# Rotary angles and half of the mask work moved from VectorE to GpSimd in a two-layer decoder trunk

## The chip, the cores and the metric

The kernel runs on one core of a Trainium2 chip. The metric is the device time of one execution in microseconds (us), the median of several runs. The engines are named as the profile names them: PE is TensorE (its matmuls; PEld its weight loads), DVE is VectorE, ACT is ScalarE, POOL is GpSimd, SP the engine whose queue issues most of the DMAs. Each engine works through its own queue in order and waits on semaphores of the others.

## The reference

256 tokens of width 1024 pass through two layers. Each layer is, cut to what matters:

```python
mod = silu(c) @ w_ada + b_ada              # shift, scale, gate
h   = rms_norm(x, pre_g) * (1 + scale) + shift
proj = h @ w_in                            # q k v g of branch A, q k v g of branch B
q, k = apply_partial_rope(q, cos, sin)     # first 16 of 64 head dims, angle = position * inv_freq
o   = attention(q, k, v) * silu(g)         # A: dilated windows mixed; B: causal at this length
x   = x + gate * rms_norm(concat(o_a, o_b) @ w_out, post_g)
```

All arithmetic is float32. The rotary angles come from integer positions up to some 4,350, and the cosines and sines are shared by both layers. Branch A adds to its scores a mask that counts in how many of three dilated windows a key lies; branch B adds a causal mask. Both masks depend on nothing but the distance of query and key.

## The kernel before

**Tiling.** 128 tokens are one tile (t = 0, 1); the width 1024 is eight blocks of 128. Every float32 matrix product is made of three products of rounded parts: a weight piece `raw` (128 x 1024, 512 KB, seven buffers) is loaded by SP, rounded to `whi` on ACT (L205), and the rest `wlo = raw - whi` is formed on DVE in two instructions of 128 x 512 (L212). The activations have `hi` (ACT) and `lo` (DVE) in the same way. A `raw` buffer is loaded again when its readers are done.

**Order.** Up to the end of the first part of layer 0 the order of all engines is that of the program text (`manual_schedule`), and the string FIRST_STEPS sets it: each word is a step. The steps that matter here:

- `n0`, `n1` (`first_norm`, L698): sum of squares of a token tile on ACT (L702), reciprocal root on POOL in two instructions (L462, L465), scaling on DVE (L704) into `oo` (tile 0) or `acc_ss` (tile 1).
- `T0` (`small_inputs`, L273): one PE transpose (L275) of the small inputs into a PSUM tile `t`, from which ACT makes `cs` = silu(c) (L276) and DVE makes `csz`, `posf` (positions) and `cols` (L277 to L279).
- `x0`, `x1` (`first_x`, L707): eight PE transposes of a scaled token tile (L712), in two groups of four into one PSUM tile each, and the copies of the two tiles on ACT (L713). For token tile 0 the PSUM tiles are of the name `t`, of which there are two buffers.
- `k3`, `k1` (`keep_clock`, L793): three matmuls, or one, of 128 x 512 whose result nobody reads (L797).
- `a0`, `m0`: matmuls of w_ada for a group of columns (L414), the copy on ACT (L418), two or four transposes (L370), and shift and scale `mod` on DVE (L426, L375, L376); `a1`, `m1` and so on for the next groups.
- `h10`, `l10` and so on (`first_h`, `first_lo`): `hf` on DVE (L724), `hi` on ACT (L726), `lo` on DVE (L734). `g02`: the two L212 halves of a piece in part. `p02`: six matmuls of w_in (L753). `w00`, `y00`: splits of whole pieces. `s00`, `v00`: matmuls on those (L513).
- `R0`, `R1`, `R2` (`make_rope`, L284): R0 fills two small constants on POOL (L288, L292: 8 and 9 memsets of one column) and forms the angles of the positions, 7 instructions on DVE (L296 to L302, 128 x 16); R1 reduces them to turns, 18 instructions on DVE (L307 to L324, 128 x 16 to 128 x 48); R2 is four Sin instructions on ACT (L328 to L331). The results are first read where q and k of layer 0 are taken out of PSUM (L547).
- `K1` (`make_masks`, L252 to L258): eight DVE instructions of 128 x 384 that finish the masks `mka` and `mkb`. The first part of the masks (L246 to L250) is made on DVE before the first norm. The masks are first read at L601, after st_S of the first head pair.

From there on PE's order is written out and the other engines' order comes from the scheduler.

Of the kernel before, what the change touches and what calls it, by code (L numbers as in the profile page):

```python
# [21 lines left out]
BIG = 1e30  # L22
# [20 lines left out]

GROUPS = ((0, 1), (1, 1), (2, 2), (4, 2), (6, 2))
FIRST_LOADS = 'a0 f01 f00 a1 s00 b2 a2 f10 s01 f11 v00 a3 b3 v01 f20 a4 f21 f30 b4 f31'
FIRST_STEPS = """n0 T0 R0 k3 n1 x0 R1 k1 a0 f00 f01 x1 m0 h00 h01 l00 g00 l01 g01 a1 f02 m1 p00 f03 p01 h10 h11 l10
g02 R2 l11 g03 p02 w00 s00 a2 b2 m2 p03 f10 h20 h21 g10 l20 l21 f11 f12 g11 s02 f13 g12 g13 w01 K1
p10 p11 a3 s01 s03 p12 y00 y01 b3 p13 m3 f20 h30 h31 l30 g20 f21 l31 v00 f22 f23 g21 g22 g23 v01 p20
p21 a4 f30 g30 f31 g31 b4 p22 m4 p23 h40 h41 l41 l40 v02 f32 f33 v03 g32 g33 p30 p31 p32 p33"""
GATE_AT = (21, 27)  # L50
# [24 lines left out]
def trunk(ctx: ExitStack, tc: tile.TileContext, x, c, positions, pre_gain, post_gain,  # L75
          w_ada, b_ada, w_in, w_out, out):
    nc = tc.nc
# [4 lines left out]
    NT = S // P  # L82
# [85 lines left out]
    for x in FIRST_LOADS.split():  # L168
        i, g, m = x[0], int(x[1]), int(x[2:] or 0)
# [67 lines left out]
    def make_masks():  # L237
        dist = ap.tile([P, NS], I32, name="z", bufs=4)
        nc.gpsimd.iota(dist[:, 0:P], pattern=[[-1, P]], base=0, channel_multiplier=1)
        nc.gpsimd.iota(dist[:, P:NS], pattern=[[-1, S]], base=P, channel_multiplier=1)  # L240
        d = dist
        mka, mkb = masks
        tmi = ap.tile([P, NS], I32, name="z", bufs=4)
        tmf = ap.tile([P, NS], F32, name="z", bufs=4)
        cnt = ap.tile([P, NS], F32, name="z", bufs=4)
        nc.vector.tensor_scalar(cnt, d, 128.0, None, op0=ALU.is_le)  # L246
        for m in (3, 15):
            nc.vector.tensor_scalar(tmi, d, m, None, op0=ALU.bitwise_and)
            nc.vector.tensor_scalar(tmf, tmi, 0.0, None, op0=ALU.is_equal)
            nc.vector.tensor_add(cnt, cnt, tmf)  # L250
        yield
        nc.vector.tensor_scalar(mkb, d, 0.0, BIG, op0=ALU.is_lt, op1=ALU.mult)  # L252
        nc.vector.tensor_scalar(tmf, d, 0.0, None, op0=ALU.is_ge)
        nc.vector.tensor_mul(cnt, cnt, tmf)
        nc.vector.tensor_scalar(mka, cnt, 0.0, BIG, op0=ALU.is_equal, op1=ALU.mult)
        for v in (2, 3):
            nc.vector.tensor_scalar(tmf, cnt, float(v), -math.log(v), op0=ALU.is_equal, op1=ALU.mult)
            nc.vector.tensor_add(mka, mka, tmf)  # L258
        yield

# [23 lines left out]
    def make_rope():  # L284

        invf = cp.tile([P, RH], F32, name="invf")
        for i in range(RH):
            nc.gpsimd.memset(invf[:, i:i + 1], INV_FREQ[i])  # L288
        tcn = cp.tile([P, 3, 3], F32, name="tcn")
        for j, r in enumerate(turn_constants()):  # L290
            for i in range(3):
                nc.gpsimd.memset(tcn[:, i, j:j + 1], r[i])  # L292
        NA = NT * RH
        ang = cp.tile([P, 4, NA], F32, name="ang")
        pcs = cp.tile([P, 3, NA], F32, name="pcs")
        nc.vector.tensor_mul(ang[:, 0, :].rearrange("p (t i) -> p t i", t=NT),  # L296
                             posf[:, :, None].to_broadcast([P, NT, RH]),
                             invf[:, None, :].to_broadcast([P, NT, RH]))
        for j, e in enumerate((20, 8, -4)):
            mg = 1.5 * 2.0 ** (23 + e)  # L300
            nc.vector.tensor_scalar(pcs[:, j, :], ang[:, j, :], mg, mg, op0=ALU.add, op1=ALU.subtract)
            nc.vector.tensor_sub(ang[:, j + 1, :], ang[:, j, :], pcs[:, j, :])  # L302
        yield
        RND = 1.5 * 2.0 ** 23
        tp = cp.tile([P, 3, 3, NA], F32, name="tp")
        for i in range(3):
            nc.vector.tensor_mul(tp[:, i], pcs, tcn[:, i, :, None].to_broadcast([P, 3, NA]))  # L307
        rr = cp.tile([P, 3, NA], F32, name="rr")
        nc.vector.tensor_scalar(rr, tp[:, 0], RND, RND, op0=ALU.add, op1=ALU.subtract)
        nc.vector.tensor_sub(rr, tp[:, 0], rr)  # L310
        nc.vector.tensor_add(tp[:, 1], tp[:, 1], tp[:, 2])
        sm = cp.tile([P, 4, NA], F32, name="sm")
        nc.vector.tensor_add(sm[:, 0, :], rr[:, 0, :], rr[:, 1, :])
        nc.vector.tensor_add(sm[:, 0, :], sm[:, 0, :], rr[:, 2, :])
        nc.vector.tensor_scalar(sm[:, 2, :], sm[:, 0, :], RND, RND, op0=ALU.add, op1=ALU.subtract)
        nc.vector.tensor_sub(sm[:, 0, :], sm[:, 0, :], sm[:, 2, :])
        nc.vector.tensor_add(sm[:, 1, :], tp[:, 1, 0, :], tp[:, 1, 1, :])
# [3 lines left out]
        nc.vector.tensor_add(sm[:, 0, :], sm[:, 0, :], sm[:, 1, :])
        nc.vector.tensor_scalar_add(sm[:, 1, :], sm[:, 0, :], 0.25)
        nc.vector.tensor_scalar(sm[:, 2:4, :], sm[:, 0:2, :], RND, RND, op0=ALU.add, op1=ALU.subtract)
        nc.vector.tensor_sub(sm[:, 0:2, :], sm[:, 0:2, :], sm[:, 2:4, :])  # L324
# [516 lines left out]
    for l in range(L):  # L841
# [27 lines left out]
        for n, (ci, hf, t) in enumerate(slots):  # L869
            i = n + 32 - len(slots)  # L870
# [58 lines left out]
```

## Time and profile before

| | us |
|---|---|
| median of three runs (315.86 to 316.15) | 316.12 |
| the profiled execution | 315.87 |
| its span, first to last instruction | 313.8 |
| PE busy | 295.8 (94%) |
| DVE busy | 244.9 (78%) |
| ACT busy | 203.5 (65%) |
| POOL busy | 12.8 (4%) |
| DMA, queue 1, mean share of 16 engines | 66.2% |

Busy time is a sum over the whole span; in which stretch an engine holds up the others is read from the chain that ended last and from the waits. PE's 94% does not mean that its array works at its peak: a matmul's record runs until its result is out, so that records overlap. The spacing of the starts tells the pace. Idle time of an engine which nobody waits for costs nothing.

### The profile page before, as it was taken

Reading aid. Unit: us, or ns where it says so; the run is one execution under the profiler, and the core shown is the slowest. Engines: PE = TensorE matmul, PEld = TensorE weight load, DVE = VectorE, ACT = ScalarE, POOL = GpSimd, SP = SyncE. Lnnn points to the kernel's source line nnn. Section 1 sums busy time; section 2 is a strip of 40 time slices with the busy share of each in tenths; the row PEclk is TensorE's granted clock in tenths of the full one; section 3 lists DMA queues with packets and bytes.
Section 4 is the critical chain, followed back from the end, with each engine's and each line's share of the span. In section 5 each row is a group of like instructions: output and inputs, shape, how many; then the busy total and the mean of one; then the engine's idle time right before and its main releaser. Section 6 shows DMA issues by size and latency. Waiting matters only on the chain.

```text
span 313.8 us, 5291 instructions
## 1 busy us (share of the span) xinstructions
PE 295.8 (94%) x1817; PEld 237.6 (76%) x1817; DVE 244.9 (78%) x637; ACT 203.5 (65%) x435; POOL 12.8 (4%) x46
## 2 busy tenths in 40 slices
PE   0989999989999999999999899999999999999992
PEld 0666576868777799997787688878777799997881
DVE  4775874999999999999689899979965566776122
ACT  3555253969597479988387376569776579984100
POOL 3100001000010000000021200000000000000001
PEclk9999999999999999999999999999999999999997
DMA  7999998999789877687946649988754441000011
GB/s 253 341 361 363 335 359 276 341 351 318 274 291 278 285 269 218 232 284 248 314 164 222 212 138 327 359 311 264 233 169 136 134 137 66 2 1 2 0 67 67
DMA packets 37394, 70.63 MB, mean 225 GB/s; under 512 B 2492, under 2 KB 12790, under 8 KB 37368
## 3 DMA queue, kind: packets, MB, share of 16 engines
q1 hardware_dynamic: 36960, 69.22, 66.2%
q10 hardware_dynamic: 408, 1.09, 1.0%
q8 instruction: 14, 0.23, 0.3%
q14 instruction: 12, 0.10, 0.1%
HBM read 69.24 MB, written 1.05 MB: 224 GB/s over the span
## 4 chain that ended last, share of the span: by engine, by line
PE 85%; DVE 5%; ACT 5%; issue 1%; POOL 1%; ACTq 1%; DVEq 0%; POOLq 0%
PE mm L513 41%; PE mm L526 15%; PE o L642 4%; PE mm L753 4%; PE t L625 4%; PE t L513 3%; PE t L571 3%; PE o L414 3%; DVE wlo L212 2%; PE s L592 2%; PE s L595 2%; ACT whi L205 1%; PE s L753 1%; PE s L513 1%; PE t L370 1%
## 5 line engine op out<-in xcount | busy, mean ns | idle before, releaser
L212 DVE TENSOR_TENSOR wlo<-raw,whi 128x512 fp32r<-128x512 f32 x160 | 102.7, 687 | 11.6 <-PE mm L513 4.5
L205 ACT ACTIVATE whi<-raw 128x1024 fp32r<-128x1024 f32 (+1 forms) x88 | 84.0, 978 | 21.5 <-DMA raw<-in_w_in_dram 11.5
L513 PE MATMUL mm<-whi,hi 128*128 128x512 f32 x200 | 81.4, 407 | 0.0
L513 PE MATMUL mm<-whi,lo 128*128 128x512 f32 x200 | 79.0, 395 | 0.0
L513 PE MATMUL mm<-wlo,hi 128*128 128x512 f32 x200 | 79.0, 395 | 0.0
L513 PEld LDWEIGHTS mm<-whi,hi 128*128 128x128 f32 x200 | 37.6, 188 | 10.2 <-issue 1.7
L513 PEld LDWEIGHTS mm<-wlo,hi 128*128 128x128 f32 x200 | 37.6, 188 | 8.8
L513 PEld LDWEIGHTS mm<-whi,lo 128*128 128x128 f32 x200 | 37.7, 189 | 8.1 <-DVE lo L502 0.3
L526 PE MATMUL mm<-hi,whi 128*128 128x256 f32 x128 | 36.9, 288 | 0.0
L526 PE MATMUL mm<-hi,wlo 128*128 128x256 f32 x128 | 36.0, 281 | 0.0
L526 PE MATMUL mm<-lo,whi 128*128 128x256 f32 x128 | 36.0, 281 | 0.0
L604 ACT ACTIVATE z<-z,den 128x128 f32<-128x128 f32 x64 | 28.4, 448 | 4.7 <-DVE den L601 4.6
L526 PEld LDWEIGHTS mm<-hi,whi 128*128 128x128 f32 x128 | 24.1, 188 | 0.7 <-issue 0.2
L526 PEld LDWEIGHTS mm<-lo,whi 128*128 128x128 f32 x128 | 24.1, 188 | 0.2
L526 PEld LDWEIGHTS mm<-hi,wlo 128*128 128x128 f32 x128 | 24.1, 188 | 0.0
L364 DVE SCALAR_TENSOR_TENSOR acc_g<-raw,cs,acc_g 128x1024 f32<-128x1024 f32 x16 | 20.5, 1282 | 0.6 <-DMA raw<-in_w_ada_dram 0.5
L687 DVE TENSOR_TENSOR oo<-mm,gate 128x512 f32<-128x512 f32 x8 | 5.5, 690 | 17.7 <-ACT qk L685 17.6
L685 ACT ACTIVATE qk<-mm 128x512 f32<-128x512 f32 x8 | 4.7, 593 | 21.8 <-PE mm L513 21.8
L364 DVE SCALAR_TENSOR_TENSOR acc_ss<-raw,cs,acc_ss 128x1024 f32<-128x1024 f32 x14 | 17.6, 1276 | 0.0
L628 ACT ACTIVATE pT<-t 128x384 f32<-128x384 f32 x32 | 14.0, 490 | 0.2
L642 PE MATMUL o<-pT,vv 128*64 128x128 f32 x192 | 14.0, 281 | 0.0
L625 PE MATMUL t<-ident,z 128*128 128x128 f32 x96 | 13.4, 276 | 0.0
(173 smaller groups left out, 451.7 us busy)
## 6 DMA issues: line engine op xcount, KB each, us to landing
raw<-in_w_in_dram SPq DMA_DIRECT2D x64, 512.0 KB, 5.3
raw<-in_w_ada_dram SPq DMA_DIRECT2D x32, 512.0 KB, 5.1
raw<-in_w_ada_dram SPq DMA_DIRECT2D x32, 256.0 KB, 5.5
raw<-in_w_out_dram SPq DMA_DIRECT2D x16, 512.0 KB, 5.0
xs<-in_x_dram SPq DMA_DIRECT2D x2, 512.0 KB, 4.2
gate<-in_post_norm_gain_dram ACTq DMA_DIRECT2D x2, 512.0 KB, 5.0
out_dram<-xs SPq DMA_DIRECT2D x4, 256.0 KB, 2.1
rows<-in_b_ada_dram ACTq DMA_DIRECT2D x2, 8.0 KB, 5.0
```

What stands on the lines that cost most here:

```text
L205: nc.scalar.activation(hi_q[key][:, a:b, :], raw[:, a:b, :], AF.Copy)
L212: nc.vector.tensor_sub(lo[:, d, :], raw[:, d, :], hi[:, d, :].bitcast(F32))
L364: nc.vector.scalar_tensor_tensor(a[:, sl], r[:, sl], cs[:, k:k + 1], a[:, sl], op0=ALU.mult, op1=ALU.add)
L414: nc.tensor.matmul(pm[32 * j:32 * j + 32, :w], csz[:, k, :], r[:, i * w:(i + 1) * w], start=k < 4, stop=k >= 4, tile_position=(0, 32 * j))
L513: nc.tensor.matmul(bank, a[:, k, t, :], w[:, k % 2, :], start=first and k + i == 0, stop=last and k == KH - 1 and i == 2)
L526: nc.tensor.matmul(bank[:, b * S:(b + 1) * S], w[:, k % 2, c0:c0 + P], a[:, k].rearrange("p t q -> p (t q)"), start=hf + b + k + i == 0, s ...
L571: nc.tensor.transpose(pt[:, (2 * i + t) * P:(2 * i + t + 1) * P], qk[br, i][:, t, p * P:(p + 1) * P], ident)
L604: nc.scalar.activation(z[:, a:b], z[:, a:b], AF.Exp, bias=den[:, 0, t, i:i + 1], scale=-1.0, accum_out=den[:, 1, t, i:i + 1])
L625: nc.tensor.transpose(pt[:, b * P:(b + 1) * P], pp[i][:, b * P:(b + 1) * P], ident)
L628: nc.scalar.activation(d, pt[:, :NS], AF.Copy)
L642: nc.tensor.matmul(ob[i * HD:(i + 1) * HD, q0:q0 + P], v[:, t, h], res[i][:, c0:c0 + P], start=t == 0, stop=n != 1, tile_position=(0, i * HD))
L753: nc.tensor.matmul(mm[0, ci, t], a[:, k, t, :], w[:, ci, :], start=q == 0 and j == 0 and i == 0, stop=q == 3 and j == 1 and i == 2)
```

## The change

The seven angle instructions of R0, the 18 of R1 and the eight of K1 go from DVE to POOL. One DVE instruction that multiplied and added (L319) becomes two on POOL, so that R1 has 19 there. The steps are put in another order: both norms come first, R0, R1 and K1 follow `T0` at once, R2 moves from behind `g02` to the place that K1 had, and the step `k1`, one matmul of `keep_clock`, is no longer in the list.

```diff
-FIRST_STEPS = """n0 T0 R0 k3 n1 x0 R1 k1 a0 f00 f01 x1 m0 h00 h01 l00 g00 l01 g01 a1 f02 m1 p00 f03 p01 h10 h11 l10
-g02 R2 l11 g03 p02 w00 s00 a2 b2 m2 p03 f10 h20 h21 g10 l20 l21 f11 f12 g11 s02 f13 g12 g13 w01 K1
+FIRST_STEPS = """n0 n1 T0 R0 R1 k3 K1 x0 a0 f00 f01 x1 m0 h00 h01 l00 g00 l01 g01 a1 f02 m1 p00 f03 p01 h10 h11 l10
+g02 l11 g03 p02 w00 s00 a2 b2 m2 p03 f10 h20 h21 g10 l20 l21 f11 f12 g11 s02 f13 g12 g13 w01 R2
...
-        nc.vector.tensor_scalar(mkb, d, 0.0, BIG, op0=ALU.is_lt, op1=ALU.mult)
+        nc.gpsimd.tensor_scalar(mkb, d, 0.0, BIG, op0=ALU.is_lt, op1=ALU.mult)
...
-        nc.vector.tensor_mul(ang[:, 0, :].rearrange("p (t i) -> p t i", t=NT),
+        nc.gpsimd.tensor_mul(ang[:, 0, :].rearrange("p (t i) -> p t i", t=NT),
...
-        nc.vector.scalar_tensor_tensor(sm[:, 1, :], ang[:, 3, :], 1.0 / (2.0 * math.pi), sm[:, 1, :],
-                                       op0=ALU.mult, op1=ALU.add)
+        nc.gpsimd.tensor_scalar(ang[:, 3, :], ang[:, 3, :], 1.0 / (2.0 * math.pi), None, op0=ALU.mult)
+        nc.gpsimd.tensor_add(sm[:, 1, :], ang[:, 3, :], sm[:, 1, :])
```

On PE, between the transposes of token tile 0 and the first matmuls of w_ada, with the semaphores that each row waits for (DVE, Activation and Pool are counts of those engines, DMAHW counts of DMAs), before:

```order
L797 MATMUL s<-onesr 128x512 x2
L712 MATMUL t<-ident,oo 128x128 [waits DVE_49]
L712 MATMUL t<-ident,oo 128x128 x3
L712 MATMUL t<-ident,oo 128x128 [waits DVE_49,Activation_49]
L712 MATMUL t<-ident,oo 128x128 x3
L797 MATMUL s<-onesr 128x512
L414 MATMUL o<-raw,csz 32x256 [waits DMAHW7_49,DMAHW0_49,Pool_49]
```

and after the change:

```order
L797 MATMUL s<-onesr 128x512 x2
L712 MATMUL t<-ident,oo 128x128 [waits DVE_49]
L712 MATMUL t<-ident,oo 128x128 x3
L712 MATMUL t<-ident,oo 128x128 [waits Activation_49]
L712 MATMUL t<-ident,oo 128x128 x3
L414 MATMUL o<-raw,csz 32x256 [waits DMAHW0_49,DMAHW7_49,DVE_49,Pool_49]
```

The single L797 is gone. The second group of transposes waits for another count of ACT: before it was the one reached with `cs` (L276), the reader of the PSUM tile of `T0`; in the changed program it is the one reached with the first L713, the reader of the tile that the first group of four has just written. The two groups now share one buffer of `t`, and the tile of `T0` keeps the other until the transposes of `m0` (L370), which wait for `cols` (L279).

On POOL, from the first norm on (`+` stands only in the changed program, `-` only in the one before; after the last row shown the angle instructions go on, and the eight of the masks follow):

```order
 L462 TENSOR_SCALAR rstd<-ms 128x1
 L465 TENSOR_TENSOR rstd<-rstd,nhalf 128x1
+L462 TENSOR_SCALAR rstd<-ms 128x1
+L465 TENSOR_TENSOR rstd<-rstd,nhalf 128x1
 L288 MEMSET invf 128x1 x8
 L292 MEMSET tcn 128x1 x9
-L462 TENSOR_SCALAR rstd<-ms 128x1
-L465 TENSOR_TENSOR rstd<-rstd,nhalf 128x1
+L296 TENSOR_TENSOR ang<-posf,invf 128x16
+L301 TENSOR_SCALAR pcs<-ang 128x16
+L302 TENSOR_TENSOR ang<-ang,pcs 128x16
```

The second norm has moved ahead of the constants, and 26 angle and eight mask instructions stand where the queue was empty until the memset of `acc_g` (L352).

On DVE, at the scaling of the token tiles:

```order
 L704 TENSOR_SCALAR oo<-xs,rstd 128x1024
+L704 TENSOR_SCALAR acc_ss<-xs,rstd 128x1024
 L277 COPY csz<-cs 128x8
 L278 COPY posf<-t 128x2
 L279 COPY cols<-t 128x48
-L296 TENSOR_TENSOR ang<-posf,invf 128x16
-L301 TENSOR_SCALAR pcs<-ang 128x16
-L302 TENSOR_TENSOR ang<-ang,pcs 128x16
```

The scaling of tile 1 has moved ahead of the three small copies, and the next instruction after `cols` is now L426 of `m0`. All later rows of DVE, but for the eight of the masks, are those of before.

## Rows read from the trace of the kernel before

**Rows 1.** PE's waits (total us, times, longest us), and one stretch of the windows.

```profile
PE t L275 <- DVE oo L704: 7.8, 1, 7.8
PE t L370 <- ACT hf L418: 1.3, 2, 0.7
PE t L571 <- DVE qk L550: 1.0, 1, 1.0
...
100.00:150.00 50.00, 50.00 (x401) 43.41 (x399) 48.06 (x115) 40.63 (x89) 0.00 (x0) 1.00 0.79 258
```

**Rows 2.** PE in the timeline at the start: start us, duration us, what.

```profile
7.82 0.33 PE L275 MATMUL t<-ident,rows 58*128 58x58 f32 x1 [7.82 <-DVE oo L704]
...
9.53 1.91 PE L712 MATMUL t<-ident,oo 128*128 128x128 f32 x8
11.09 0.78 PE L797 MATMUL s<-onesr 128*128 128x512 f32 x1
11.79 1.81 PE L414 MATMUL o<-raw,csz 128*32 128x256 f32 x16
13.53 1.09 PE L712 MATMUL s<-ident,acc_ss 128*128 128x128 f32 x8
...
17.33 0.47 PE L753 MATMUL mm<-whi,hi 128*128 128x512 f32 x1
```

**Rows 3.** ACT and DVE in the timeline of the same stretch.

```profile
8.48 0.15 DVE L278 COPY posf<-t 128x2 f32<-128x2 f32 x1
...
10.62 0.60 ACT L713 ACTIVATE acc_g<-t 128x512 f32<-128x512 f32 x1 [1.22 <-PE t L712]
...
14.88 0.17 DVE L426 TENSOR_REDUCE mod<-t 128x2 f32<-128x8 f32 x1 [0.80 <-PE t L370]
```

**Rows 4.** POOL in the timeline: a norm's two instructions.

```profile
5.80 0.22 POOL L462 TENSOR_SCALAR rstd<-ms 128x1 f32<-128x1 f32 x1 [3.57 <-ACT oo L702]
6.11 0.57 POOL L465 TENSOR_TENSOR rstd<-rstd,nhalf 128x1 f32<-128x1 f32 x1
```

**Rows 5.** POOL beside DVE: line L724 (ns min/median/max), then pieces of the timeline.

```profile
L724 DVE TENSOR_SCALAR hf<-gate,mod x8: 341/346/1056, 15.8 to 52.2; 128x128 f32<-128x128 f32 x8
...
52.19 1.02 POOL L352 MEMSET acc_g<- 128x1024 f32 x1 [41.80 <-DVE hf L724]
...
173.78 2.49 DVE L212 TENSOR_TENSOR wlo<-raw,whi 128x512 fp32r<-128x512 f32 x4
174.72 1.72 POOL L464 TENSOR_SCALAR rstd<-ms 128x1 f32<-128x1 f32 x1 [2.31 <-ACT oo L481]
...
9.80 0.59 POOL L465 TENSOR_TENSOR rstd<-rstd,nhalf 128x1 f32<-128x1 f32 x1
9.99 0.18 DVE L302 TENSOR_TENSOR ang<-ang,pcs 128x16 f32<-128x16 f32 x1
```

**Rows 6.** DVE from m1 to w00 in the timeline, and the matmul that reads g02's product.

```profile
17.92 0.16 DVE L426 TENSOR_REDUCE mod<-t 128x2 f32<-128x8 f32 x1
...
19.31 0.29 DVE L734 TENSOR_TENSOR lo<-hf,hi 128x128 fp32r<-128x128 f32 x1
19.52 0.68 DVE L212 TENSOR_TENSOR wlo<-raw,whi 128x512 fp32r<-128x512 f32 x1
...
20.32 1.92 DVE L212 TENSOR_TENSOR wlo<-raw,whi 128x512 fp32r<-128x512 f32 x3
...
20.67 0.40 PE L753 MATMUL mm<-wlo,hi 128*128 128x512 f32 x1
...
26.62 0.17 DVE L426 TENSOR_REDUCE mod<-t 128x4 f32<-128x16 f32 x1 [4.38 <-PE t L370]
```

**Rows 7.** The matmuls of w_ada for a2 and for a4 in the timeline.

```profile
23.10 2.14 PE L414 MATMUL o<-raw,csz 128*32 128x512 f32 x16
...
46.87 1.93 PE L414 MATMUL o<-raw,csz 128*32 128x512 f32 x16
```

**Rows 8.** First and last of K1's eight DVE instructions, and m4 on DVE.

```profile
32.55 0.35 DVE L252 TENSOR_SCALAR mkb<-z 128x384 f32<-128x384 int32 x1
...
35.46 0.56 DVE L258 TENSOR_TENSOR mka<-mka,z 128x384 f32<-128x384 f32 x1
...
50.86 0.17 DVE L426 TENSOR_REDUCE mod<-t 128x4 f32<-128x16 f32 x1 [3.93 <-PE t L370]
```

**Rows 9.** ACT's wait behind the split of w01.

```profile
36.54 1.06 ACT L205 ACTIVATE whi<-raw 128x1024 fp32r<-128x1024 f32 x1 [4.28 <-DMA raw<-in_w_in_dram]
```

More of the change, by code (lines that the diff above doesn't have):

```diff
@@ L251, in make_masks @@
         yield
-        nc.vector.tensor_scalar(mkb, d, 0.0, BIG, op0=ALU.is_lt, op1=ALU.mult)
-        nc.vector.tensor_scalar(tmf, d, 0.0, None, op0=ALU.is_ge)
-        nc.vector.tensor_mul(cnt, cnt, tmf)
-        nc.vector.tensor_scalar(mka, cnt, 0.0, BIG, op0=ALU.is_equal, op1=ALU.mult)
+        nc.gpsimd.tensor_scalar(mkb, d, 0.0, BIG, op0=ALU.is_lt, op1=ALU.mult)
+        nc.gpsimd.tensor_scalar(tmf, d, 0.0, None, op0=ALU.is_ge)
+        nc.gpsimd.tensor_mul(cnt, cnt, tmf)
+        nc.gpsimd.tensor_scalar(mka, cnt, 0.0, BIG, op0=ALU.is_equal, op1=ALU.mult)
         for v in (2, 3):
-            nc.vector.tensor_scalar(tmf, cnt, float(v), -math.log(v), op0=ALU.is_equal, op1=ALU.mult)
-            nc.vector.tensor_add(mka, mka, tmf)
+            nc.gpsimd.tensor_scalar(tmf, cnt, float(v), -math.log(v), op0=ALU.is_equal, op1=ALU.mult)
+            nc.gpsimd.tensor_add(mka, mka, tmf)
         yield
@@ L300, in make_rope @@
             mg = 1.5 * 2.0 ** (23 + e)
-            nc.vector.tensor_scalar(pcs[:, j, :], ang[:, j, :], mg, mg, op0=ALU.add, op1=ALU.subtract)
-            nc.vector.tensor_sub(ang[:, j + 1, :], ang[:, j, :], pcs[:, j, :])
+            nc.gpsimd.tensor_scalar(pcs[:, j, :], ang[:, j, :], mg, mg, op0=ALU.add, op1=ALU.subtract)
+            nc.gpsimd.tensor_sub(ang[:, j + 1, :], ang[:, j, :], pcs[:, j, :])
         yield
@@ L306, in make_rope @@
         for i in range(3):
-            nc.vector.tensor_mul(tp[:, i], pcs, tcn[:, i, :, None].to_broadcast([P, 3, NA]))
+            nc.gpsimd.tensor_mul(tp[:, i], pcs, tcn[:, i, :, None].to_broadcast([P, 3, NA]))
         rr = cp.tile([P, 3, NA], F32, name="rr")
-        nc.vector.tensor_scalar(rr, tp[:, 0], RND, RND, op0=ALU.add, op1=ALU.subtract)
-        nc.vector.tensor_sub(rr, tp[:, 0], rr)
-        nc.vector.tensor_add(tp[:, 1], tp[:, 1], tp[:, 2])
+        nc.gpsimd.tensor_scalar(rr, tp[:, 0], RND, RND, op0=ALU.add, op1=ALU.subtract)
@@ L312, in make_rope @@
+        nc.gpsimd.tensor_sub(rr, tp[:, 0], rr)
+        nc.gpsimd.tensor_add(tp[:, 1], tp[:, 1], tp[:, 2])
         sm = cp.tile([P, 4, NA], F32, name="sm")
[L313 to L317, printed above, removed]
@@ L318, in make_rope @@
-        nc.vector.tensor_add(sm[:, 1, :], sm[:, 1, :], tp[:, 1, 2, :])
-        nc.vector.scalar_tensor_tensor(sm[:, 1, :], ang[:, 3, :], 1.0 / (2.0 * math.pi), sm[:, 1, :],
-                                       op0=ALU.mult, op1=ALU.add)
[L321 to L324, printed above, removed]
+        nc.gpsimd.tensor_add(sm[:, 0, :], rr[:, 0, :], rr[:, 1, :])
@@ new lines, in make_rope @@
+        nc.gpsimd.tensor_add(sm[:, 0, :], sm[:, 0, :], rr[:, 2, :])
+        nc.gpsimd.tensor_scalar(sm[:, 2, :], sm[:, 0, :], RND, RND, op0=ALU.add, op1=ALU.subtract)
+        nc.gpsimd.tensor_sub(sm[:, 0, :], sm[:, 0, :], sm[:, 2, :])
+        nc.gpsimd.tensor_add(sm[:, 1, :], tp[:, 1, 0, :], tp[:, 1, 1, :])
+        nc.gpsimd.tensor_add(sm[:, 1, :], sm[:, 1, :], tp[:, 1, 2, :])
+        nc.gpsimd.tensor_scalar(ang[:, 3, :], ang[:, 3, :], 1.0 / (2.0 * math.pi), None, op0=ALU.mult)
+        nc.gpsimd.tensor_add(sm[:, 1, :], ang[:, 3, :], sm[:, 1, :])
@@ L325, in make_rope @@
+        nc.gpsimd.tensor_add(sm[:, 0, :], sm[:, 0, :], sm[:, 1, :])
+        nc.gpsimd.tensor_scalar(sm[:, 1, :], sm[:, 0, :], 0.25, None, op0=ALU.add)
+        nc.gpsimd.tensor_scalar(sm[:, 2:4, :], sm[:, 0:2, :], RND, RND, op0=ALU.add, op1=ALU.subtract)
+        nc.gpsimd.tensor_sub(sm[:, 0:2, :], sm[:, 0:2, :], sm[:, 2:4, :])
         yield
```

## The prediction

> **What bounds the kernel now.** I read PE's waits first, then the stretches, then the timeline of the first 27 us. After the start PE waits little: its longest totals are 1.3 us for the copy ahead of L370 and 1.0 us for the rotary of q and k ahead of the first attention transposes, and from 100 to 150 us it is busy for 50.00 of 50 us [rows 1]. So the time is PE's work plus whatever delays it, and a delay at the start is kept to the end unless one of those waits takes it up. The change acts only on the first 36 us. There the reader should look for two things: who holds PE before its first long row of matmuls at 17.33 us [rows 2], and how little time lies between a DVE product and the matmul that reads it right after [rows 6].
>
> That DVE is relieved is no gain by itself. The angle work of R1 lies in front of 14.88 us, where DVE then still waits 0.80 us for PE [rows 3]. K1 occupies DVE from 32.55 to 36.02 us; the next DVE work on which PE later waits begins at 50.86 us, behind an idle time of 3.93 us that PE's transposes end [rows 8]. I price the relief at nothing; what hides it is this idle time.
>
> **Part 1: the steps in front of w_ada.** The transpose of the small inputs starts at 7.82 us [rows 2]. The profile names DVE's L704 as its releaser [rows 1], but in the program it waits for DVE's first copy and for DMAs, so the second L704, now in front of the small copies, does not hold it. The two groups of four transposes of `x0` now share a PSUM buffer, so the second group waits for the copy of the first. That copy starts at 10.62 and takes 0.60 us [rows 3], which gives 11.22, or 11.26 us with a handover of 0.04. Eight transposes with the start of the next work took 1.56 us (9.53 to 11.09), 0.195 us each [rows 2]; four take 0.78, and w_ada's matmuls can start at 12.04 instead of 11.79 us. The removed L797, worth 0.70 us (11.09 to 11.79), is in this number: without the new wait its removal would have been a gain of that size. **Part 1 costs 0.25 us**, between nothing (if the w_ada matmuls run faster for starting later) and 0.5.
>
> PE's clock is granted as 1.00 in every stretch of the records [rows 1], which would be 2.4 GHz. Yet eight transposes take 1.91 us at 9.53 and 1.09 us at 13.53 [rows 2], so PE becomes about twice as fast between these, after working without a break since 7.82 us. The change puts a pause of some 0.6 us into that stretch. I take the rise to come at the same time; the other answer is a rival below.
>
> **Part 2: POOL beside DVE.** The 26 angle instructions start when `posf` exists: 8.48 us plus 0.15 before [rows 3], now behind the second L704, so some 0.6 us later, 9.2 us. A small dependent POOL instruction takes 0.31 us from start to start (5.80 to 6.11), at most 0.57 like the power instruction [rows 4]. At 0.31 they need 8.1 us and end at 17.3 us; at 0.57, 14.8 us and 24.0 us. Sin, their only reader, now stands behind w01 on ACT, where ACT then waits 4.28 us, to 36.54 us [rows 9]: room at either pace, so moving R2 costs nothing.
>
> The eight mask instructions of 128 x 384 follow. No row has one on POOL. One column costs 0.22 us [rows 4] and a memset of 1024 columns 1.02 us [rows 5], so 384 columns come to about 0.52 us where one input is read; for the three with two inputs I estimate 0.5 to 0.8, and take 0.65. Five and three make 4.6 us, from 17.3 to 21.9 us.
>
> What this does to DVE is bounded by [rows 5]. Upwards: an L724 of 0.346 us took 1.056 while POOL's memset ran from 52.19, so DVE can stand still for a whole POOL instruction. The other way round, POOL's L464 took 1.72 us behind a row of L212 which left no gap. Downwards: DVE's L302 at 9.99 us took 0.18 us, its usual time, while POOL's L465 ran from 9.80 to 10.39. So I take big POOL instructions to hold DVE in each gap of its queue, small ones not at all.
>
> The Trainium skill (page "SBUF — State Buffer", section "SBUF: two separate sides") goes further: VectorE and GpSimd share one pair of ports, whichever starts takes it for its whole instruction, and this counts for a VectorE instruction with two SBUF inputs against any GpSimd instruction that reads SBUF. The 0.18 us row does not show this for small instructions; the rule would add the price of the second rival below.
>
> Mask instructions from 17.3 us meet the chain of m1: L426 at 17.92, then L375, L376 and the first L724, each waiting for the one before it, then L734 at 19.31 and g02's L212 at 19.52 [rows 6]. Before that, the L212 of g00 and g01 leave no gap. I count three gaps, ahead of L375, L376 and L724: half of one POOL instruction, a whole one and one with two inputs, 0.25 + 0.5 + 0.65 = 1.4 us. What covers part of it is g02's slack: it ends at 20.20 and its matmul starts at 20.67 [rows 6], so 0.47 us. **Part 2 costs 0.9 us**, between nothing and 1.9 (all three gaps at full length and a fourth ahead of L734). The rest of the masks finds DVE without gaps (L212 up to 22.24 us) and then idle for 4.38 us to 26.62 [rows 6], where it hurts nobody.
>
> **Given back.** Sixteen L414 of 512 columns took 2.14 us at 23.10 and 1.93 at 46.87 [rows 7]. If the difference is waiting for loads, a later PE does not wait: **0.2 us back**, between nothing and 0.2.
>
> **The sum.** 0.25 + 0.9 - 0.2 = +0.95 us. On the profiled execution (span 313.8, 315.87 us with what lies around it) this gives 316.8; it lay 0.25 us below the median of the runs shown, so the median becomes 316.12 + 0.95 = 317.1 us.
>
> **The rivals.**
>
> *The masks miss the chain (not slower).* If the angle instructions take over 0.44 us each, (20.7 - 9.2) / 26, the masks begin when DVE is in its row of L212 without a gap, and run in its 4.38 us of idle time [rows 6]. The same holds if big POOL instructions hold DVE as little as the small one did. Then 0.25 - 0.2 is left: 316.2 us, 316.0 to 316.5. For it: 0.57 us is a POOL instruction with two inputs, and over half of the angle instructions have two. Against it: that one is a power. With angles over 0.57 us the masks would reach m2 at 26.62 us and the cost returns.
>
> *Small instructions hold DVE too.* Then m0's five dependent DVE instructions behind 14.88 us [rows 3] also wait, up to 0.22 us each (L462 [rows 4]): 0.5 to 1.1 us more, 317.6 to 318.2. Against it stands the 0.18 us row.
>
> *PE's faster pace comes later.* The pause falls into the only stretch in which PE earned it. `x1` alone would take 0.8 us more (1.91 against 1.09 [rows 2]), and the rows behind it likewise: +1 to +2.5 us on the sum's first part, 317.5 to 319. The Trainium skill (page "TensorE: Matmul & The Clock Gate", Part 1, "What's actually happening") has a clock gate that looks at how busy the engine has recently been, which is the same direction; the granted clock of 1.00 does not show it.
>
> *The relief pays after all (faster).* K1's 3.47 us on DVE delay the release of `raw` buffers. If earlier loads let DVE start its work ahead of L571 sooner, up to PE's wait of 1.0 us [rows 1] comes back: 315.2 to 315.9. Against it: 50.86 us, which is PE's own time.
>
> **How the numbers follow.** About 0.2% (0.6 us, so 315.5 and 316.7) is what a measurement of this kernel can tell from no change. Forecast 0.45 (316.6 to 317.8; 0.43 slower, 0.02 same); masks miss the chain 0.27 (0.24 same, 0.03 faster); small instructions hold DVE 0.12, slower; the pace comes later 0.10, slower; the relief pays 0.06, faster. Slower 0.65, same 0.26, faster 0.09. The range reaches from the lower end of the case without collision, 316.0, to 318.5, through the second rival and the cheaper half of the third; what is left out is the gain (0.06) and the dearest ends.
>
> **What would show it.** In the profile after: the second four transposes of `x0` starting some 0.04 us after the end of the first L713, near 11.3 us; w_ada's first matmul near 12.0; POOL's masks between 17 and 22 us; L375, L376 or L724 of m1 stretched by 0.3 us or more, with g02's matmul late by about 1.1 us; PE's later waits unchanged. It would be wrong if these stretches are not there (then the time stays at 316.2), if the transposes of `x1` still take 1.9 us, or if the wait ahead of L571 shrinks.

## The result, and the profile after

The changed kernel takes 319.05 us (median of 5 runs, 318.41 to 319.73), the kernel before, run beside it, 315.86 (315.46 to 316.15). The ratio is 1.0097, 95% interval 1.0086 to 1.0108: **3.1 us slower**. The forecast was +0.95 us, 317.1, with a range to 318.5. The sign was right, and so were two places where time is lost; the size was too small by a factor of three. Two much longer executions, one of 742 us in e9 and one of 586 us in e10, are left out of the times and ratios below.

The profiled execution took 319.12 us, span 317.3 (before: 315.87, span 313.8). From the page after: the engines' busy time, then the shares of the chain that ended last.

```profile
span 317.3 us, 5290 instructions
...
PE 298.2 (94%) x1816; PEld 237.6 (75%) x1816; DVE 239.1 (75%) x605; ACT 203.8 (64%) x435; POOL 30.1 (9%) x79
...
PE 84%; DVE 6%; ACT 3%; DMA 2%; issue 2%; POOL 1%; DVEq 0%; POOLq 0%; SPq 0%; ACTq 0%
```

PE's waits after (total us, times, longest us) answer to [rows 1]:

```profile
PE t L275 <- DMA raw<-in_w_ada_dram: 8.7, 1, 8.7
...
PE t L370 <- ACT hf L418: 1.7, 2, 0.9
...
PE t L571 <- DVE qk L550: 1.0, 1, 1.0
...
PE t L712 <- ACT acc_g L713: 0.7, 1, 0.7
```

One wait is new, 0.7 us ahead of L712; the wait ahead of L571 is what it was. PE's timeline at the start (start us, duration us), which answers to [rows 2]:

```profile
8.66 0.33 PE L275 MATMUL t<-ident,rows 58*128 58x58 f32 x1 [8.66 <-DMA raw<-in_w_ada_dram]
...
10.37 1.06 PE L712 MATMUL t<-ident,oo 128*128 128x128 f32 x4
12.11 1.12 PE L712 MATMUL t<-ident,oo 128*128 128x128 f32 x4 [0.69 <-ACT acc_g L713]
13.16 1.93 PE L414 MATMUL o<-raw,csz 128*32 128x256 f32 x16
15.02 1.97 PE L712 MATMUL s<-ident,acc_ss 128*128 128x128 f32 x8
...
19.87 0.48 PE L753 MATMUL mm<-whi,hi 128*128 128x512 f32 x1
...
26.56 1.92 PE L414 MATMUL o<-raw,csz 128*32 128x512 f32 x16
```

Two things are to be seen. The second four transposes of `x0` wait 0.69 us for the copy of the first four. And `x1`, the eight transposes at 15.02, takes 1.97 us, where before it took 1.09 [rows 2]: PE has not yet reached its faster pace there. The prediction had named this as a sign that it would be wrong.

DVE's timeline from m1 to w00, which answers to [rows 6]:

```profile
20.66 0.27 DVE L375 TENSOR_TENSOR mod<-mod,cols 128x2 f32<-128x2 f32 x1
...
21.23 0.44 DVE L724 TENSOR_SCALAR hf<-acc_g,mod 128x128 f32<-128x128 f32 x1
...
22.04 0.81 DVE L734 TENSOR_TENSOR lo<-hf,hi 128x128 fp32r<-128x128 f32 x1 [0.21 <-ACT hi L726]
22.78 0.68 DVE L212 TENSOR_TENSOR wlo<-raw,whi 128x512 fp32r<-128x512 f32 x1
23.38 0.58 DVE L734 TENSOR_TENSOR lo<-hf,hi 128x128 fp32r<-128x128 f32 x1
```

L734 takes 0.81 and 0.58 us, where its usual time is 0.29 [rows 6]. PE's weight loads show who waits for that (start, duration, what, wait):

```profile
22.91 0.19 PEld L753 LDWEIGHTS mm<-whi,lo 128*128 128x128 f32 x1 [0.20 <-DVE lo L734]
23.51 0.19 PEld L753 LDWEIGHTS mm<-wlo,hi 128*128 128x128 f32 x1 [0.41 <-DVE wlo L212]
...
24.02 0.19 PEld L753 LDWEIGHTS mm<-whi,lo 128*128 128x128 f32 x1 [0.21 <-DVE lo L734]
...
25.22 0.19 PEld L513 LDWEIGHTS s<-wlo,hi 128*128 128x128 f32 x1 [0.44 <-DVE wlo L212]
...
26.13 0.19 PEld L513 LDWEIGHTS s<-wlo,hi 128*128 128x128 f32 x1 [0.38 <-DVE wlo L212]
```

And POOL's timeline, the cause beside it:

```profile
10.59 0.21 POOL L296 TENSOR_TENSOR ang<-posf,invf 128x16 f32<-128x16 f32 x1 [0.83 <-DVE cols L279]
10.89 0.30 POOL L301 TENSOR_SCALAR pcs<-ang 128x16 f32<-128x16 f32 x1
...
17.90 0.25 POOL L324 TENSOR_TENSOR sm<-sm 128x32 f32<-128x32 f32 x1
18.24 1.60 POOL L252 TENSOR_SCALAR mkb<-z 128x384 f32<-128x384 int32 x1
19.90 1.68 POOL L253 TENSOR_SCALAR z<-z 128x384 f32<-128x384 int32 x1
21.67 1.04 POOL L254 TENSOR_TENSOR z<-z 128x384 f32<-128x384 f32 x1
22.80 2.04 POOL L255 TENSOR_SCALAR mka<-z 128x384 f32<-128x384 f32 x1
...
29.29 1.01 POOL L258 TENSOR_TENSOR mka<-mka,z 128x384 f32<-128x384 f32 x1
```

The angles keep the forecast pace (26 in 7.56 us, 0.29 each). The eight masks are busy for 11.5 us between 18.24 and 30.30, where 4.6 were forecast. A DVE instruction beside a mask with one tensor input (TENSOR_SCALAR) loses at most 0.3 us; one that starts inside a mask with two (TENSOR_TENSOR), other than the TENSOR_REDUCE of L426, stands until that mask ends, as L734 at 22.04 beside L254, which ends at 22.71.

**Where the time went.** The table gives the time between PE rows that occur in every version: from L275's start to the first L753 (p00), to the first L414 of 512 columns (a2), to the L370 of m2, to that of m3, on to POOL's L464 of the later norm, and to the end. Then come the duration of `x1`'s eight transposes and, in the last column (clock), how long after L275's start the trace's records of TensorE's granted clock begin. In the traces of these versions the first record is at 1.00, which is 2.4 GHz, and none stands before it; the profile's views print 1.00 there as well. In front of that moment rows of PE take up to twice as long as behind it (16 L414 of 256 columns 1.93 against 1.07 us), so PE's faster pace and this record begin together.

| | L275 at | to p00 | to a2 | to m2 | to m3 | to L464 | to the end | x1 | clock |
|---|---|---|---|---|---|---|---|---|---|
| before | 7.82 | 9.51 | 5.77 | 2.82 | 14.31 | 116.89 | 156.68 | 1.09 | 5.5 |
| before, again (e14) | 7.66 | 9.79 | 5.76 | 2.67 | 14.44 | 116.87 | 156.35 | 1.28 | 6.3 |
| after | 8.66 | 11.21 | 6.69 | 2.67 | 14.95 | 116.89 | 156.26 | 1.97 | 9.4 |
| after, again (e1) | 7.24 | 10.38 | 6.97 | 2.67 | 14.90 | 116.90 | 156.24 | 1.36 | 6.9 |
| after, again (e12) | 7.56 | 11.04 | 6.70 | 2.67 | 15.14 | 116.88 | 156.25 | 1.84 | 7.9 |
| after, again (e13) | 7.75 | 11.43 | 7.57 | 2.67 | 14.48 | 116.91 | 156.36 | 1.97 | 9.6 |

Means of four profiles after against two before: +1.4 us up to p00 (11.0 against 9.65), +1.2 up to a2 (6.98 against 5.77), +0.5 between m2 and m3 (14.87 against 14.38), -0.1 and -0.2 in the stretches a2 to m2 and at the end. That sums to +2.8 us of span. The times of these same executions lie 2.5 us apart on average, less than the 3.1 us of the timed runs, so that some of the loss is in no profile. L275 starts between 7.18 and 8.66 us over all runs here, on loads, in no order that goes with a version, so the 0.84 us between the two first profiles is chance. So is the end: 156.7 and 156.3 us both occur with the kernel before.

### The profile page after: what moved, and what is told of

The parts are those of the page before. It is cut to its first block, busy times and chain, and to the rows that moved or that the text cites. A ratio compares the mean times of both kernels' runs of the same rounds, so it can differ in the third digit from the quotient of the medians.

```text
span 317.3 us, 5290 instructions
## 1 busy us (share of the span) xinstructions
PE 298.2 (94%) x1816; PEld 237.6 (75%) x1816; DVE 239.1 (75%) x605; ACT 203.8 (64%) x435; POOL 30.1 (9%) x79
## 3 DMA queue, kind: packets, MB, share of 16 engines
q10 hardware_dynamic: 408, 1.09, 0.9%
HBM read 69.24 MB, written 1.05 MB: 222 GB/s over the span
## 4 chain that ended last, share of the span: by engine, by line
PE 84%; DVE 6%; ACT 3%; DMA 2%; issue 2%; POOL 1%; DVEq 0%; POOLq 0%; SPq 0%; ACTq 0%
PE mm L513 41%; PE mm L526 15%; PE o L642 4%; PE t L625 4%; PE mm L753 3%; DVE wlo L212 3%; PE t L513 3%; PE o L414 3%; PE t L571 3%; PE s L592 2%; PE s L595 2%; DMA raw<-in_w_ada_dram 1%; PE s L513 1%; ACT whi L205 1%; DMA xs<-in_x_dram 1%
## 5 line engine op out<-in xcount | busy, mean ns | idle before, releaser
L212 DVE TENSOR_TENSOR wlo<-raw,whi 128x512 fp32r<-128x512 f32 x160 | 102.8, 685 | 15.5 <-PE mm L513 4.5
L513 PEld LDWEIGHTS mm<-whi,hi 128*128 128x128 f32 x200 | 37.6, 188 | 10.1 <-issue 1.7
L464 POOL TENSOR_SCALAR rstd<-ms 128x1 f32<-128x1 f32 x6 | 3.0, 508 | 208.7 <-ACT qk L685 203.2
```

What stands on the lines that cost most here:

```text
L212: nc.vector.tensor_sub(lo[:, d, :], raw[:, d, :], hi[:, d, :].bitcast(F32))
L513: nc.tensor.matmul(bank, a[:, k, t, :], w[:, k % 2, :], start=first and k + i == 0, stop=last and k == KH - 1 and i == 2)
```

## The experiments

The theory: the new order makes a pause in PE's early work, which delays PE's faster pace; and masks on POOL stretch DVE's small instructions at m1. Rivals: the pause costs only its own length; the missing L797 is the cause; the angles on POOL hold DVE; chance of the start.

### The changed kernel and the one before, again

No edit. Expected of e1, of the timed e9, and of the single profiles e12 to e14:

> The changed kernel, looked at a second time. In its first profile the transpose of the small inputs (L275) began at 8.66 us against 7.82 in the kernel before, because loads landed later. If that belongs to the change, L275 begins near 8.7 us again; if it is chance from execution to execution, anywhere from 7.8 to 8.7. If the pause in PE ahead of the second four transposes of x0 is what delays PE's faster pace, the transposes of x1 again take about 1.9 us; if the pace comes at a chance moment, they may take 1.1.

> The changed kernel once more, timed beside the next two on one chip. If the loss is about 3 us on any chip: 318.5 to 319.5 and 2.7 to 3.5 us over the kernel before. If the single 317.08 us of the second look was the rule there: 1 us over the kernel before.

> The changed kernel, a further look at its first 30 us. From L275 to p00 it took 11.21 and 10.38 us in the two looks so far, 9.51 in the kernel before. If the pause makes PE's pace both later and uncertain, this look lies between 10.1 and 11.8; if 11.21 was chance, near 10.4. From p00 to a2: 6.7 to 7.6 us where the masks meet m1.

> The same once more, with the same expectation: L275 to p00 10.1 to 11.8 us, p00 to a2 6.7 to 7.6 us.

> The kernel before, looked at a second time, to see how far its first 30 us move by themselves. If the pace without a pause is steady: L275 to p00 9.3 to 9.9 us, x1 1.1 us, p00 to a2 5.75 to 5.8 us. If it is as uncertain as in the changed kernel: x1 up to 1.9 us and L275 to p00 up to 11 us.

Single times: 317.08 (e1), 318.02 (e12), 318.95 us (e13), and for the kernel before 315.62 (e14) and 316.92 us, the second without a trace. Timed again (e9) the change gives 319.05 us (median of five), ratio 1.0095, interval 1.0080 to 1.0111: the first result stands.

In the column `x1` of the table the kernel before also varies (1.09 and 1.28), but less, and the changed one is at the slow pace through nearly all of `x1` in three of four profiles. Up to the first L370 (`m0`), which stands behind `x1` and in front of the first mask in all four, the mean is 7.96 us from L275 against 6.80 before: +0.53 is the later start of w_ada, the other 0.6 us the later pace. One profile is not enough to price this term.

### The order alone

From the changed kernel, masks and angles go back to DVE, and the new order stays, except that K1 stands behind w01 again (lines cut):

```diff
-FIRST_STEPS = """n0 n1 T0 R0 R1 k3 K1 x0 a0 ...
+FIRST_STEPS = """n0 n1 T0 R0 R1 k3 x0 a0 ...
...
-... g13 w01 R2
+... g13 w01 K1 R2
...
-        nc.gpsimd.tensor_scalar(mkb, d, 0.0, BIG, op0=ALU.is_lt, op1=ALU.mult)
+        nc.vector.tensor_scalar(mkb, d, 0.0, BIG, op0=ALU.is_lt, op1=ALU.mult)
...
-        nc.gpsimd.tensor_mul(ang[:, 0, :].rearrange("p (t i) -> p t i", t=NT),
+        nc.vector.tensor_mul(ang[:, 0, :].rearrange("p (t i) -> p t i", t=NT),
```

> The new order of the first steps with all angle and mask instructions on DVE (R0 and R1 directly behind the small copies, the masks at their old place); the single L797 is gone as in the change. Nothing new runs on POOL. Theory (the order alone makes the pause and the late pace): about 1.7 us over the kernel before, 317.5, and x1 takes 1.9 us. Rival (POOL's work is the whole cost): 315.9.

317.18 us, ratio 1.0043 (1.0025 to 1.0061): **+1.4 us with nothing new on POOL**. PE's timeline of e5 has the pause:

```profile
11.50 1.11 PE L712 MATMUL t<-ident,oo 128*128 128x128 f32 x4 [0.69 <-ACT acc_g L713]
12.54 1.93 PE L414 MATMUL o<-raw,csz 128*32 128x256 f32 x16
14.40 1.09 PE L712 MATMUL s<-ident,acc_ss 128*128 128x128 f32 x8
```

So the order, of which the sum had 0.25 us, costs over five times that. But the profile does not show the late pace that was expected with it: `x1` takes 1.09 us, and the clock's records begin 6.3 us after L275, as in e14. This execution took 316.68 us, 0.9 over the kernel before; it has +0.5 up to p00, the wait, and +0.5 between m2 and m3.

### Masks on DVE, angles on POOL

The edit of e5 without the lines of the angles (e4 timed, e15 one more profile):

> The changed kernel with the eight mask instructions back on DVE at their old place behind w01; the angles stay on POOL, and the order of the first steps stays. Theory (POOL's masks hold DVE in the chain of m1 and cost 0.9 us, and the later raw buffers 0.6 us more at a3): the total falls by 0.9 to 1.5 us, to 317.5 to 318.1; x1 still takes 1.9 us, and L734 of h10 takes 0.29 us instead of 0.81. Rival (the masks cost nothing, the whole loss is at the start): 319.0 and a2 as late as in the changed kernel.

> The version with the masks on DVE and the pause still there, a second look: L275 to p00 10.1 to 11.8 us as in the changed kernel, since POOL's masks begin later than that stretch; p00 to a2 5.75 to 5.8 us. If the masks on POOL have a part in the late pace, 10.4 at most.

317.04 us, ratio 1.0030 (1.0010 to 1.0050); e15 took 316.52. p00 to a2 is back at 5.77 and 5.75 us, so the whole +1.2 of that stretch belongs to the masks on POOL. Up to p00 it takes 10.41 and 10.50, still +0.8. `x1` takes 1.39 and 1.47 us, not the 1.9 expected; the clock's records begin 7.0 and 7.2 us after L275. That is earlier than in three of the four profiles of the change. The masks on POOL cannot hold the pace back there, as they begin behind the rise, or 0.2 us ahead of it in e13; why it is later with them stays open. e4 does not lie above e5, so the angles on POOL cost nothing that can be measured: the rival "small instructions hold DVE" falls. Against the change, from which it differs in the masks alone, e4 is 2.0 us faster.

### A PSUM buffer of its own for the second group

Transposes of the second group of `x0` go to another buffer, so that they need not wait. e11 is the same kernel again.

```diff
-            pt = ps.tile([P, CW], F32, name=("t", "s")[t], bufs=2)
+            pt = ps.tile([P, CW], F32, name=("t", "s")[t or g], bufs=2)
```

> The changed kernel with one edit: the second four transposes of token tile 0 write a PSUM tile of the other name, so that they no longer wait for the copy of the first four. Theory (the pause costs its own 0.5 us and delays PE's pace, 1.2 us more): x1's transposes take 1.1 us instead of 1.97, the total falls by 1.5 to 1.9 us, to about 317.3. Rival (the pace comes late because the single L797 is gone, or by chance): x1 still takes 1.9 us, and only the pause goes, 0.5 us, to about 318.5.

> The changed kernel with the second four transposes of token tile 0 in a PSUM tile of the other name, masks early on POOL, timed beside the changed kernel on one chip. Theory (pause and late pace 1.7 to 2.2 us, early masks 0.9 us): 316.8, some 2 us under the changed kernel and 0.9 us over the version with the masks held back.

316.87 us, ratio 1.0019 (1.0003 to 1.0036), and 316.78, ratio 1.0025 (1.0012 to 1.0037). The pause is gone, as the timeline of e2 shows:

```profile
10.54 1.06 PE L712 MATMUL s<-ident,oo 128*128 128x128 f32 x4
...
13.40 1.39 PE L712 MATMUL s<-ident,acc_ss 128*128 128x128 f32 x8
```

**With the masks early on POOL, over 2 of the 3.1 us go with the pause.** The theory had 1.1 us for `x1`; it is 1.39 here and 1.09 in e11, so without the pause the pace still varies, as in the kernel before; the clock's records begin 6.1 us after L275 here and 3.5 in e11.

### The pause filled

The pause stays, but PE does one more row of the filler L797 in it:

```diff
+            if g == 1 and t == 0:
+                keep_clock(1)
```

> The changed kernel with a matmul of 128x512 that nobody reads put between the two groups of four transposes of token tile 0; the second group still waits for the copy, but PE works meanwhile. Theory (idle time of PE delays its pace): w_ada's first matmul starts as late as in the changed kernel or 0.1 us later, but x1 takes 1.1 us, and the total falls by 1.0 to 1.2 us, to about 317.9. Rival (the wait itself is the cost and the pace is chance): no change, 319.0.

316.95 us, ratio 1.0021 (1.0000 to 1.0042). PE's timeline (line numbers are two higher here):

```profile
11.94 1.06 PE L714 MATMUL t<-ident,oo 128*128 128x128 f32 x4 [0.26 <-ACT acc_g L715]
12.93 1.07 PE L414 MATMUL o<-raw,csz 128*32 128x256 f32 x16
13.94 1.09 PE L714 MATMUL s<-ident,acc_ss 128*128 128x128 f32 x8
```

This run tells the theory from its nearest rival. The wait for the copy is still there, and w_ada's matmuls start as late after L275 as in the changed kernel (4.44 us against 4.50). Yet they run at the fast pace: the clock's records begin 4.3 us after L275 instead of 6.9 to 9.6. And 2.1 us come back, where 1.0 to 1.2 were expected. So it is not the delay but the idle time: what PE does in it decides when it becomes fast. The profile itself, of 317.84 us, lies 0.9 us above e3's median; up to p00 it takes 10.19 us, as PE then waits 1.45 us for pieces of w_ada.

### The filler back in its old place

The removal of the filler row between `x0` and `a0` is undone by moving the step k1:

```diff
-FIRST_STEPS = """n0 n1 T0 R0 R1 k3 K1 x0 a0 ...
+FIRST_STEPS = """n0 n1 T0 R0 R1 k3 K1 x0 k1 a0 ...
```

> The changed kernel with the single L797 back between x0 and w_ada. The pause stays. Theory (idle time of PE sets when the pace comes): w_ada starts 0.5 us later, x1 takes 1.9 us again, the total rises by 0.3 to 0.6 us, to 319.5. Rival (the missing L797 is why the pace comes late): x1 takes 1.1 us and the total falls by 0.5 to 1 us, to 318.2.

319.02 us, ratio 1.0101 (1.0076 to 1.0125), as slow as the change; the rise of 0.3 to 0.6 us that was expected does not show. Its `x1`, after a filler row behind the pause:

```profile
11.94 0.78 PE L797 MATMUL s<-onesr 128*128 128x512 f32 x1
...
14.51 1.97 PE L712 MATMUL s<-ident,acc_ss 128*128 128x128 f32 x8
```

The clock's records begin 9.0 us after L275. The same row in the pause (e3) gives back 2.1 us, behind it nothing. That the filler is missing is not the cause.

### Masks alone on POOL

The kernel before with the masks' lines on POOL and K1 ahead of k1, everything else in the old order (steps cut):

```diff
-... x0 R1 k1 a0 ...
+... x0 R1 K1 k1 a0 ...
...
-... g12 g13 w01 K1
+... g12 g13 w01
```

> The kernel before with one edit: the eight mask instructions are on POOL, behind the second norm, and nothing else is moved, so there is no pause in PE. They then start near 10.5 us and take 1 to 2 us each, so they run to about 22 us and meet m0 as well as m1. Theory (a big POOL instruction holds a DVE instruction in each gap): 0.9 to 1.8 us over the kernel before, 316.8 to 317.7, and some of L375, L376, L724 and L734 are stretched. Rival (it costs only where other delays have moved it): 315.9 to 316.2.

318.10 us, ratio 1.0064 (1.0048 to 1.0081): +2.0 us without any pause (`x1` 1.09), more than the theory's 0.9 to 1.8. With no angles in front of them the masks begin at 10.39 and meet more of DVE's work. POOL's first mask, and DVE rows beside it:

```profile
10.39 2.09 POOL L252 TENSOR_SCALAR mkb<-z 128x384 f32<-128x384 int32 x1
```

```profile
14.07 0.87 DVE L323 TENSOR_SCALAR sm<-sm 128x32 f32<-128x32 f32 x1
...
18.69 0.79 DVE L375 TENSOR_TENSOR mod<-mod,cols 128x2 f32<-128x2 f32 x1
...
21.32 1.10 DVE L734 TENSOR_TENSOR lo<-hf,hi 128x128 fp32r<-128x128 f32 x1
```

An L375 of two columns, usually 0.17 us, takes 0.79; p00 to a2 takes 7.20 us. Each of the three starts inside a mask with two inputs, which ends at 14.90, 19.46 and 22.27 us, and ends with it or up to 0.15 us behind it. What the masks cost depends on what they meet.

### Neither pause nor masks on POOL

The edits of the own buffer and of the masks on DVE together:

> The changed kernel with both cures: the second four transposes of token tile 0 in a PSUM tile of the other name, and the masks on DVE at their old place. What is left of the change: the angles on POOL, the norms first, no single L797. Theory (pause and masks are the whole cost): within 0.4 us of the kernel before, 315.5 to 316.2; if the removed L797 is then a gain of up to 0.5 us, 315.4. Rival (small POOL instructions, or the later second norm, cost as well): 316.5 or more.

315.72 us, ratio 0.9992 (0.9981 to 1.0002): the whole loss is gone, and the rest of the change (angles on POOL, both norms first) is worth nothing. It does reach p00 earlier, 9.09 us behind L275, but gives that back:

```profile
11.35 1.25 PE L414 MATMUL o<-raw,csz 128*32 128x256 f32 x16
...
22.65 2.29 PE L414 MATMUL o<-raw,csz 128*32 128x512 f32 x16
```

The second row takes 2.29 us, against 1.93 for a4's [rows 7], as if PE came too early for its loads; the profile lists no such wait there. e11 and e7 differ in the masks alone: 316.78 against 315.72, **1.1 us for the masks on POOL**.

### Masks on POOL, but late

The own buffer, and a POOL instruction ahead of the masks that reads a product of DVE, so that POOL begins them only behind the split of w01:

```diff
+        late = cp.tile([P, 1], F32, name="late")
+        nc.gpsimd.tensor_scalar(late, lo_q["in", 0, 2, 0, 1][:, 1, 0:1].bitcast(F32), 0.25, None, op0=ALU.add)
         nc.gpsimd.tensor_scalar(mkb, d, 0.0, BIG, op0=ALU.is_lt, op1=ALU.mult)
```

> The changed kernel with the second four transposes of token tile 0 in a PSUM tile of the other name, and the masks still on POOL but held back: a one-column POOL instruction in front of them reads the last product of the split of w01 on DVE, so that they start near 32 us, behind m2, and run for some 12 us while DVE first has L212 without gaps and is then idle until m3. Theory (where POOL's masks meet a chain of dependent DVE instructions is what costs, not that they run on POOL): from the first matmul of w_in (p00) to a2 5.8 us instead of 6.7 to 7.0, and the total at 315.5 to 316.0, that of the version with the masks on DVE. Rival (big POOL instructions slow DVE wherever they run): 316.5 or more, and L212 beside them longer than 0.69 us.

315.31 us, ratio 0.9984 (0.9974 to 0.9994): **0.5 us (0.16%) faster than the kernel before**, and 1.5 us faster than e11, timed beside it. From e7, with the masks on DVE, it can't be told: the intervals overlap. POOL, DVE and PE (line numbers two higher):

```profile
31.24 0.76 POOL L253 TENSOR_SCALAR late<-wlo 128x1 f32<-128x1 f32 x1 [13.05 <-DVE wlo L212]
32.08 1.83 POOL L254 TENSOR_SCALAR mkb<-z 128x384 f32<-128x384 int32 x1
...
39.51 1.01 POOL L260 TENSOR_TENSOR mka<-mka,z 128x384 f32<-128x384 f32 x1
...
42.19 1.05 POOL L260 TENSOR_TENSOR mka<-mka,z 128x384 f32<-128x384 f32 x1
```

```profile
39.66 0.87 DVE L378 SCALAR_TENSOR_TENSOR mod<-mod,cols 128x2 f32<-128x2 f32 x1
...
42.27 1.52 DVE L212 TENSOR_TENSOR wlo<-raw,whi 128x512 fp32r<-128x512 f32 x1
```

```profile
43.84 0.50 PE L755 MATMUL mm<-wlo,hi 128*128 128x512 f32 x1 [0.85 <-DVE wlo L212]
```

p00 to a2 takes 5.75 us, as expected, and the time up to m3 is no longer than before (14.18 us). But the masks are not free at the late place: L378 stands until the first L260 shown ends, and L212 takes 1.52 us beside the second, instead of 0.69. PE waits 0.85 us for that L212, and from the transposes of m3 to those of m4 this version takes 11.10 us, where each other one takes 9.99 to 10.02. So the rival's sign, a longer L212, came, though not its total. The masks cost PE 1.1 us of this trace here too. It is still a fast one because the stretches ahead are short (8.65 us up to p00, 9.09 in e7); which part of that the held masks make and which part the loads is not shown.

## Why the prediction was wrong

**What bounds the kernel** was read rightly: a delay at the start is kept, the wait ahead of L571 took nothing up, and DVE's relief from the angles was worth nothing (e7). **The places** were right as far as they went: two delays lie where the prediction put them, in front of w_ada and at m1; a third, between m2 and m3, it did not have.

**Part 1, the steps in front of w_ada (0.25 us).** The wait itself came as worked out. The time from L275's start to the first L414 grew from 3.97 to 4.50 us, 0.53 instead of 0.25: PE's wait is 0.69 us, and the four transposes behind it take 1.05 to the next start, not the 0.78 taken from half of the row of eight.

**The step that failed** is the sentence "I take the rise to come at the same time", which put the later pace at nothing in the sum. It was given 0.10 as a rival and came true. The clock's records begin 5.5 and 6.3 us after L275's start in the kernel before, 3.5 to 6.1 in the versions without the pause or with it filled, and 6.3 to 9.6 in the eight profiles with it. After, the L414 row and `x1` take 1.93 and 1.97 us, before 1.81 and 1.09 [rows 2]. The row in the pause (e3) and the buffer (e2, e11) each give back more than 2 us, with the masks left where they are. The profiles show less directly: 0.6 us up to m0's transposes on average, nothing in e5. So the pause is shown as the cause of the 2 us by the timed runs; how all of it comes about is not. The prediction also misread the clock: the 1.00 that it found "in every stretch" is no record in the first 13.3 us of the kernel before, and it hid the rise. The Trainium skill (page "TensorE: Matmul & The Clock Gate", Part 1, "What's actually happening") ties the clock to how busy the engine has been; e3 agrees in kind, 1.07 us for the L414 row against 1.93.

**Part 2, masks beside DVE (0.9 us).** The mechanism was right, and the cost 0.9 us in the first profile (p00 to a2, 6.69 against 5.77), 1.2 in the mean of four, 1.1 timed without the pause (e11 against e7) and 2.0 with it (the change against e4). But the 0.9 is right through two errors. A mask on POOL takes 1.5 to 2.0 us with one tensor input and 1.0 with two, not 0.52 and 0.65: neither the power on one column nor the memset was near to it, and the form with one input is the dearer. And DVE does not stand for each POOL instruction: beside masks with one input it lost 0.1 (L375), 0.1 (L724) and 0.3 us (the second L734), and only the mask with two inputs held it to its end, 0.5 us (the first L734). Less per instruction, over masks that last 11.5 instead of 4.6 us, gave the number. Their length also carried them past h10 into p02 and s00, where L734 and L212 make PE's weight loads wait 0.2 to 0.44 us five times.

**Given back (0.2 us).** The L414 row took 1.92 us at 26.56, as forecast; but it takes 1.92 us in the kernel before as well (e14), so that the 2.14 us belong to that one execution, and the mean gives back 0.1. **Not foreseen** is +0.5 us between m2 and m3. The L414 row ahead of m3 takes 1.95 us, where it took 1.33:

```profile
35.42 1.95 PE L414 MATMUL o<-raw,csz 128*32 128x512 f32 x8
```

It comes in e5 too (1.87 us, m2 to m3 14.87), with nothing new on POOL, and in e7 (14.74), without the pause; in e8, with pause and masks, m2 to m3 takes 14.04 us. So neither masks nor pause make it alone; loads that meet a moved PE are likely, but no run took them apart. **This stays open.**

**The rivals.** "Masks miss the chain" fell: the angles kept 0.29 us. "Small instructions hold DVE" fell: at m0, beside the last angles, L375 takes its 0.17 us:

```profile
17.66 0.17 DVE L375 TENSOR_TENSOR mod<-mod,cols 128x2 f32<-128x2 f32 x1
```

It is not true of every small instruction: the L704 that runs beside the 17 one-column memsets takes 1.01 us at 6.71 before and 1.02 at 9.29 after, the other one 0.75. "The relief pays" fell as it was put: the wait ahead of L571 is 1.0 us in e10 too, where both delays of the start are removed; where its 0.5 us come from was not measured. The forecast and "the pace comes later" were put as alternatives, with the range through half of one, while nothing kept both from happening; their prices, 0.95 and up to +2.5, together cover what came.

The parts timed apart do not quite add: order 1.4 and masks 1.1 make 2.5 of 3.1. Together they also meet each other. A late PE moves m0 under the first masks (an L724 takes 0.52 us there, at 18.39), and L275 to p00 takes 11.0 us on average, against 10.1 to 10.5 with the pause alone. How much of the 0.6 us that is was not measured. e4 shows the same from the other side: the masks cost 2.0 us with the pause and 1.1 without.

## What to carry to other kernels

Price a new wait on TensorE in its first microseconds not by its length but with the rows behind it at both paces, and if it can't be avoided, fill it with matmuls. Work given to GpSimd was not free here wherever VectorE made something beside it that TensorE waits for: early masks cost 1.1 us, and late ones still a wait of 0.85 us. One dummy read can hold such work back; before it is trusted, the whole stretch that it moves into has to be read, not only the one that it left. Two delays that can happen at once belong in the sum together, with a chance for both.

## What the runs showed of the hardware

- On 128 x 384 floats, with DVE idle, POOL's TENSOR_SCALAR with two steps took 1.50 us and TENSOR_TENSOR 1.01; DVE took 0.35 and 0.56 for such instructions [rows 8]. The Trainium skill (page "GPSIMD Engine Reference", section 4.1, "Engine selection") has GpSimd about two times slower with two inputs, which agrees (1.8), and near line rate with one, which these runs do not show (4.3 times); the measurement decides.
- With a pause of 0.69 us in PE's early work, the records of TensorE's granted clock (at 1.00, 2.4 GHz) begin 6.3 to 9.6 us after PE's first matmul in eight profiles; without it, or with a matmul in it, 3.5 to 6.3 us in eight others. Where no record stands, the views print 1.00 all the same.
- A TENSOR_SCALAR mask of 1.2 to 2.1 us on POOL stretched DVE instructions beside it by up to 0.3 us. A TENSOR_TENSOR mask, 1.0 us alone, held a DVE instruction that started inside it until it ended: 0.94 instead of 0.17 us (L375, e13), 0.87 instead of 0.16 (L378, e10), 1.52 instead of 0.69 (L212, e10); only the TENSOR_REDUCE L426 kept its time. The angle instructions of 0.2 to 0.3 us stretched none of the three DVE instructions of m0 beside them (0.16 and 0.17 us).
